# One closing barrier in place of two, and a last wait that subtracts its own count, in a row-maximum kernel

## Chip, cores, metric

One core of one Trainium2 chip. The metric is the device time of the core in microseconds. Beside it stands the span of the profile, which is the time from the first to the last instruction that the profile draws; the two differ. Every run in this document is on record as of the fast state, with a granted TensorE clock of 1.0, which is full speed.

## The reference

```python
def setup_inputs():
    return {"x": np.random.randn(8192, 8192).astype(np.float32)}

def reference(x):
    return np.linalg.norm(x, ord=np.inf, axis=1)
```

That is the largest absolute value of each of the 8192 rows: 268 MB to read, 32 KB to write.

## The kernel before

SyncE issues all loads, VectorE reduces each tile with an absolute maximum, and two stores write the result: the large part's from the queue of ScalarE (ACT) while the last tiles come in, the tail's from SyncE after the last reduction.

```python
        if j == len(LAST) - 4:
            ins = nc.scalar.dma_start(out=out_b, in_=r_bulk[:])     # semaphore 102
            after(ins, done, mybir.DependencyClass.Sync)
    nc.sync.dma_start(out=out_t, in_=r_tail[:])                     # semaphore 103
    nc.at_finalize(start_first_load_early)
    nc.at_finalize(finish_on_pool)
```

```python
def finish_on_pool(nc):
    sp, pool = mybir.EngineType.SP, mybir.EngineType.Pool
    body, end = nc.main_func.blocks[-2:]
    ...                                   # find the last store's semaphore: lane
    insts = end.instructions
    src = next(i for i in insts if i.engine == sp)
    at = next(k for k, i in enumerate(insts) if type(i).__name__ == "InstISA")
    drain, clear = insts[at - 1], insts[at]
    ...
    waits = sorted(src.sync_info.on_wait, key=lambda s: s.id == lane)
    wait = mybir.InstDrain(
        name=nc.get_next_instruction_name(), engine=pool, ins=[], outs=[],
        sync_info=mybir.SyncInfo(on_wait=waits, on_update=[]),
    )
    moved = {src.name, drain.name, clear.name}
    end.instructions = [i for i in insts if i.name not in moved] + [wait, clear]
```

The build splits this wait for nine semaphores into four waits for two semaphores each and a drain that waits for the ninth, VectorE's count (99). The view of line bacc.py:44 shows the four (43 ns each).

Of the kernel before, what the change touches and what calls it, by code (L numbers as in the profile page):

```python
# [62 lines left out]
                return  # L63


def finish_on_pool(nc):



    sp, pool = mybir.EngineType.SP, mybir.EngineType.Pool  # L70
    body, end = nc.main_func.blocks[-2:]
    last_store = [
        i
        for i in body.instructions
        if i.engine == sp and type(i).__name__ == "InstDMACopy"
    ][-1]
    lane = last_store.sync_info.on_update[0].id
    insts = end.instructions
    src = next(i for i in insts if i.engine == sp)
    assert type(src).__name__ == "InstDrain" and not src.sync_info.on_update  # L80
    at = next(k for k, i in enumerate(insts) if type(i).__name__ == "InstISA")
    drain, clear = insts[at - 1], insts[at]
    assert drain.engine == clear.engine == pool
    assert type(drain).__name__ == "InstDrain"
    assert not (drain.sync_info and drain.sync_info.on_wait)
    waits = sorted(src.sync_info.on_wait, key=lambda s: s.id == lane)
    assert waits[-1].id == lane
    wait = mybir.InstDrain(
        name=nc.get_next_instruction_name(),
        engine=pool,  # L90
        ins=[],
        outs=[],
        sync_info=mybir.SyncInfo(on_wait=waits, on_update=[]),
    )
    moved = {src.name, drain.name, clear.name}
    end.instructions = [i for i in insts if i.name not in moved] + [wait, clear]


@with_exitstack
def kernel(  # L100
# [101 lines left out]
    nc.sync.dma_start(out=out_t, in_=r_tail[:])  # L202
    nc.at_finalize(start_first_load_early)
    nc.at_finalize(finish_on_pool)


# [28 lines left out]
```

## Time and profile before

| | |
|---|---|
| time, median of the first 3 runs | 627.68 us (627.46 to 627.82) |
| span of the profile | 625.7 us |
| loads' queue, share of the 16 DMA engines' span | 99.5% |
| VectorE busy | 88% |
| last store: issue, landing | 624.049, 625.469 us |

In the profile's lines POOL is GpSimd, SP SyncE, ACT ScalarE, DVE VectorE and PE the tensor engine (PEld its weight loads); a q behind the name is the engine's sequencer, to which the views give the drains, the waits, the clears and the DMA issues, and L and a number is a source line. The page is read from the top: the share of the engines, the share of the DMA queues, then the chain that ended last; after that the last microseconds one instruction at a time. The prediction below shows those lines. Two lines are added here. The first is from the view of waits and says what VectorE waited for (total us, times, longest): the loads, and nothing else of size (the next entry is 0.9 us).

```profile
DVE r_bulk L140 <- DMA t<-in_x_dram: 69.7, 24, 21.0
```

The second pair is from the view of one source line, the line to which all barrier instructions belong (count, durations in ns, first and last start in us). SyncE's two drains are its entries into the two closing barriers, 0.36 us apart; the first took 123 ns, behind the store's issue, and the second 7.

```profile
L230 SPq DRAIN  x2: 7/65/123, 624.5 to 624.8; - x2
L230 SPq EVENT_SEMAPHORE  x2: 17/17/17, 624.7 to 625.0; - x2
```

No printed view lists the semaphores' updates. They are in the trace, and where the text gives three decimals of a microsecond they are read from its records one by one.

### The profile page before, as it was taken

What the parts mean: (1) busy time and instruction counts of PE and PEld (TensorE: products, weight loads), DVE (VectorE), ACT (ScalarE), POOL (GpSimd) and SP (SyncE); (2) the same over time, 40 slices, a digit from 0 to 9 for tenths busy, and PEclk for the clock granted to TensorE, in tenths of its full rate; (3) what the DMA queues carried; (4) which work ended last, traced back from release to release, by engine and by line L of the source; (5) the groups of instructions that cost most, each with busy time, mean ns of one, the idle gap of its engine ahead of it and who ended that gap; (6) DMA issues with size and microseconds to landing.
All of it is one profiled execution on the core that took longest, in us unless ns stands there. A gap on an engine that the chain in (4) does not pass through costs nothing.

```text
span 625.7 us, 205 instructions
## 1 busy us (share of the span) xinstructions
DVE 552.9 (88%) x67; POOL 0.2 (0%) x4
## 2 busy tenths in 40 slices
DVE  0588988889988889888898888988889999999998
POOL 0000000000000000000000000000000000000000
DMA  9999999999999999999999999999999999999997
GB/s 402 469 402 452 419 452 419 448 423 436 436 419 452 411 461 402 469 402 469 402 469 402 461 411 452 419 448 423 444 413 421 444 425 431 436 425 430 424 422 315
DMA packets 9282, 268.49 MB, mean 429 GB/s; under 512 B 1856, under 2 KB 1856, under 8 KB 3392
## 3 DMA queue, kind: packets, MB, share of 16 engines
q1 hardware_dynamic: 8496, 268.45, 99.5%
q10 hardware_dynamic: 784, 0.02, 0.1%
q14 instruction: 2, 0.02, 0.0%
HBM read 268.44 MB, written 0.03 MB: 429 GB/s over the span
## 4 chain that ended last, share of the span: by engine, by line
DMA 67%; DVE 31%; issue 1%; another core or an unknown queue 0%; DVEq 0%; SPq 0%
DMA t<-in_x_dram 67%; DVE r_bulk L140 24%; DVE part L140 6%; DVE t L140 2%; DVEq L230 0%; DVE r_tail L140 0%; SPq L159 0%
## 5 line engine op out<-in xcount | busy, mean ns | idle before, releaser
L140 DVE TENSOR_REDUCE r_bulk<-t 128x2 f32<-128x16384 f32 x24 | 413.3, 17220 | 69.7 <-DMA t<-in_x_dram 69.7
L140 DVE TENSOR_REDUCE part<-t 128x1 f32<-128x8192 f32 (+20 forms) x28 | 121.5, 4410 | 0.3 <-DMA t<-in_x_dram 0.3
L140 DVE TENSOR_REDUCE t<-t 128x1 f32<-128x1664 f32 (+8 forms) x11 | 16.7, 1576 | 0.2 <-DMA t<-in_x_dram 0.2
L140 DVE TENSOR_REDUCE r_tail<-t 128x1 f32<-128x644 f32 (+1 forms) x2 | 1.5, 814 | 0.0
L137 DVE MEMSET part<- 128x56 f32 x1 | 0.1, 105 | 0.9 <-PEq L219 0.9
L140 DVE TENSOR_REDUCE r_tail<-part 128x14 f32<-128x56 f32 x1 | 0.2, 201 | 0.0
L219 POOL MEMSET const-bfloat16-1.0<- 128x1 bf16 x1 | 0.1, 101 | 0.0
L219 POOL MEMSET const-uint8-127<- 128x1 uint8 x1 | 0.1, 101 | 0.0
L219 POOL MEMSET const-float32-0.0<- 128x1 f32 x1 | 0.1, 98 | 0.2 <-issue 0.2
L219 POOL MEMSET const-float32-1.0<- 128x1 f32 x1 | 0.1, 98 | 0.0
## 6 DMA issues: line engine op xcount, KB each, us to landing
t<-in_x_dram SPq DMA_DIRECT2D x2, 3392.0 KB, 37.2
t<-in_x_dram SPq DMA_DIRECT2D x1, 5376.0 KB, 40.5
t<-in_x_dram SPq DMA_DIRECT2D x1, 4864.0 KB, 32.9
t<-in_x_dram SPq DMA_DIRECT2D x1, 4800.0 KB, 32.9
t<-in_x_dram SPq DMA_DIRECT2D x1, 4672.0 KB, 34.7
t<-in_x_dram SPq DMA_DIRECT2D x3, 1536.0 KB, 36.9
t<-in_x_dram SPq DMA_DIRECT2D x1, 3520.0 KB, 42.7
t<-in_x_dram SPq DMA_DIRECT2D x1, 3328.0 KB, 40.4
```

The source lines that it names most:

```text
L137: nc.vector.memset(part[:], 0.0)
L140: return nc.vector.reduce_max(out=o, in_=i, axis=X, apply_absolute_value=True)
L219: nc = _bacc.Bacc("TRN2", target_bir_lowering=False, num_devices=1)
```

## The change

The intent: end the kernel as soon as the last store has landed. One barrier goes, GpSimd waits only for semaphores that no other instruction has already waited for at their last value (the two stores), clears all others while the last store is in flight, and the wait for that store takes its own 128 off.

```diff
-    waits = sorted(src.sync_info.on_wait, key=lambda s: s.id == lane)
-    wait = mybir.InstDrain(... on_wait=waits ...)
+    met = {}
+    for i in body.instructions:
+        for s in i.sync_info.on_wait if i.sync_info else []:
+            met[s.id] = max(met.get(s.id, 0), s.wait_value)
+    waits = [s for s in src.sync_info.on_wait if met.get(s.id, 0) < s.wait_value]
+    last = [s for s in waits if s.id == lane]
+    others = [s for s in waits if s.id != lane]
 ...
+    tail = [wait([s], []) for s in others]
+    for a, b in ((lo, lane - 1), (lane + 1, hi)):
+        if a <= b:
+            tail.append(clear_range(nc, clear, a, b))
+    reset = mybir.SyncUpdate(sync_type="semaphore", id=lane, ...,
+        update_mode="sem-sub-imm", update_value=last[0].wait_value)
+    tail.append(wait(last, [reset]))
-    moved = {src.name, drain.name, clear.name}
-    end.instructions = [i for i in insts if i.name not in moved] + [wait, clear]
+    end.instructions = [i for i in insts[: at - 1] if i.name != src.name] + tail
```

(Cut: assertions, the arguments that `...` stands for, `clear_range`, which copies the clear with another range, and `wait`, which builds a waiting instruction on GpSimd. `insts[: at - 1]` is the closing block up to the end of its first barrier.)

## The prediction

> **What bounds the kernel now.** I read the page first, then the chain of work that ended last, then the last five microseconds in order of time, and then the records of the closing instructions and of the semaphores one by one. The page:

> ```profile
> span 625.7 us, 205 instructions
> DVE 552.9 (88%) x67; POOL 0.2 (0%) x4
> ...
> q1 hardware_dynamic: 8496, 268.45, 99.5%
> ...
> HBM read 268.44 MB, written 0.03 MB: 429 GB/s over the span
> ...
> DMA 67%; DVE 31%; issue 1%; another core or an unknown queue 0%; DVEq 0%; SPq 0%
> ```

> The loads fill the 16 DMA engines for 99.5% of the span: 268.4 MB have to come in, and nothing in the change touches a load or a reduction. So some 622 of the 625.7 us are out of its reach, and only what follows the last load can move. The end of the chain of waits and the last instructions in order of time (columns: start, duration, what):

> ```profile
> 622.48 0.59 DVE r_tail L140
> 623.07 0.08 issue
> 623.15 0.87 DVEq L230
> ```

> ```profile
> 621.73 0.41 ACTq L200 DMA_DIRECT2D out_dram<-r_bulk  x1
> 622.48 1.55 DVE L140 TENSOR_REDUCE r_tail<-t 128x1 f32<-128x644 f32 x2
> 624.05 0.35 SPq L202 DMA_DIRECT2D out_dram<-r_tail  x1
> ```

> The last reduction ends at 622.48 + 1.55 = 624.03 us, and SyncE starts the last store at 624.05. The chain as printed stops there, with VectorE; it does not follow the store. The list of DMA issues does, from issue to landing:

> ```profile
> out_dram<-r_tail SPq DMA_DIRECT2D x1, 8.0 KB, 1.4
> ```

> The semaphore records make that exact: the sixteenth and last increment of this store's semaphore (103) comes at 625.469, 1.42 us after its issue. Beside it run the closing barriers, here by line and engine (durations in ns, then first and last start in us):

> ```profile
> L230 POOLq EVENT_SEMAPHORE  x4: 17/17/17, 624.6 to 625.0; - x4
> L230 PEldq EVENT_SEMAPHORE  x2: 51/51/51, 624.7 to 625.1; - x2
> L230 POOLq EVENT_SEMAPHORE_RANGE_CLEAR  x1: 92/92/92, 625.6 to 625.6; - x1
> ```

> ```profile
> bacc.py:44 POOLq EVENT_SEMAPHORE  x4: 43/43/43, 625.1 to 625.5; - x4
> ```

> One by one: the first barrier is gathered by GpSimd at 624.601 and released at 624.680; the second is gathered at 624.929 and released at 625.007, so it costs 0.328 us. GpSimd's four waits for pairs of semaphores start at 625.103, 625.195, 625.281 and 625.492; then comes a drain that waits for VectorE's count, which has no record, and the clear from 625.642 to 625.734, which is the end of the span. The fourth wait is the one that held: the three before it follow each other at about 0.09 us, so it would have started at about 625.37, but it started at 625.492, 23 ns after the last increment of semaphore 103. The store's landing, not the barriers, released the end, with about 0.12 us to spare.

> [...] the fourth wait is recorded as 43 ns, although GpSimd stood at it for about 0.12 us. So I read waits from starts and not from durations. [...] This store took 1.42 us for 8 KB and the other one 2.0 us[...]; its own packets run from 624.890 to about 625.10, and the increments come 0.2 to 0.4 us later. [...] semaphore 2 moves at 625.347 and 625.381, then not until 626.261, then four times at 23 to 99 ns; the resets run from 626.446 to 627.109. The pause ends 0.527 us after GpSimd's clear. So the runtime's closing part most likely stands waiting for GpSimd, and what ends GpSimd earlier ends the run earlier by as much.

> **The change part by part.**

> 1. The second closing barrier goes: eight instructions on the other four engines and three on GpSimd. On GpSimd alone it costs 0.328 us, but all of it lies between 624.68 and 625.07, while the store is in flight until 625.469. Worth on the path: 0.

> 2. GpSimd's waits for eight DMA semaphores and VectorE's count become two, those of the two stores. The three waits that pass at once (3 x 0.09 = 0.27 us) also lie before 625.469: 0. The drain for VectorE's count stands behind the landing: it goes, and with it most of the stretch from 625.492 to 625.642 (0.150 us).

> 3. The range clear (0.092 us on record) goes from behind the landing to before it, split in two, for 99 to 102 and 104 to 107. After the only barrier GpSimd is free at about 624.76; the first store's semaphore was complete at 623.726, so this wait passes at once, and two clears at about 0.1 us end near 625.0. That is 0.47 us before the landing: 0.

> 4. The last wait, for semaphore 103, takes its own count off. It should start where the fourth wait starts now, 23 ns after the landing, at 625.492, and the barrier waits of GpSimd that wait and subtract take 17 ns. So it ends at about 625.51, where the kernel before ended at 625.734: 0.225 us less. Counted by spacing instead, GpSimd's own instructions in the barrier follow each other at 79 to 81 ns, so the next could start at about 625.57, against 625.734 or a little later: 0.16 us or more.

> Sum: 0 + 0 + 0 + 0.16 to 0.24; I take 0.20 us. The time is 627.68 - 0.20 = 627.48 us, that is 0.03% less. In front of the last reduction nothing moves: the instruction streams of all five engines are the same up to the closing block, line numbers apart.

> **The rivals.** First, the barrier is on the path after all: a reader who adds up what is removed gets 0.328 + 0.27 + 0.24 = 0.84 us and 626.84 us. Against it speaks the fourth wait's start 23 ns behind the landing. It would hold in part if the store landed early in other executions: the 0.12 us of spare is all that could then show in the time before.

> Second, the runtime's barrier is held by something other than GpSimd's last instruction, for instance by a fixed piece of work, [...]that starts when the barrier ends. Of the pause to 626.261, 0.527 us lie behind the clear, while the first other engine signed 0.28 us after the second barrier, so GpSimd's tail is about 0.25 us longer and I cannot see what is in it. Then the gain would be 0 (627.68 us), or up to the 0.33 us by which the other engines now arrive earlier (627.35 us).

> Third, the shift is lost in the spread: the three runs before span 627.46 to 627.82 us, 0.36 us, more than the gain. [...] I think this is what the plain times will look like: no difference that three runs can tell.

> Fourth, a loss: a subtracting wait, or clears while a store is in flight, slow the store or GpSimd. The clears leave 103 alone, and semaphore updates of the barriers run beside the store's packets today, so I give it little.

> **Range and chances.** The centre is 627.48. The spread of three runs gives 0.2 us either way around a median, another session may add as much, and the rivals reach from 626.84 to about 627.7. I take 627.05 to 627.9. Two per cent would be 12.6 us, sixty times the gain; no rival comes near it, so within 2% gets 0.994, and the rest is split.

> **What would show it right or wrong.** The loads' queue should still be at 99.5%, and the last store should issue about 0.02 us after the last reduction and land 1.4 us later. The increments of semaphore 103 should be followed within about 25 ns by its fall to zero, and the clears of 99 to 102 and 104 to 107 should come before them, near 624.9 to 625.0. Semaphore 2's pause should end sooner after the landing: it was 626.261 - 625.469 = 0.79 us, and I expect about 0.59. If that difference stays at 0.79, the second rival holds; if the landing itself comes later after the issue, the fourth.

> One trap in reading it: the two clears and the last wait are built without a source position, as the drain without a record was, and the span is taken over instructions that have one. So I expect the page to print a span of about 624.8 us (the tensor engine's barrier wait, 624.734 + 0.051) and 205 - 11 - 4 - 1 = 189 instructions. Of that fall of 0.95 us only about 0.2 us is time; the rest is a tail that is no longer drawn. The run's time, not the span, decides. I am wrong if fast runs of the two kernels side by side differ by more than about 0.5 us either way.

The marks stand for cuts: general statements about records, transfers and the steps behind a kernel that were not read from this case's traces, a cause given for the spread that no run tested, and a kind of work named in the second rival. 0 + 0 + 0 + 0.16 to 0.24 us, taken as 0.20, is worked out from the trace alone. What the text calls the runtime's closing part is a group of updates at the end of the trace, described with the result. That it waits for GpSimd was inference from one number, the pause that ends 0.527 us after GpSimd's clear.

## The result

| | before | changed |
|---|---|---|
| time, median of 6 runs | 627.51 us (627.37 to 627.82) | 627.46 us (627.23 to 627.83) |
| ratio | | 0.9999 (95%: 0.9986 to 1.0012) |
| span of the profiled run | 625.7 us | 624.7 us |
| time of the profiled run | 627.57 us | 627.34 us |

A ratio is the mean time of one kernel's fast runs over the mean of the other's in the same rounds, so it is not quite the ratio of the medians in the table. By the plain times the two kernels can't be told apart. The changed kernel's page (header, queues, chain):

```profile
span 624.7 us, 189 instructions
DVE 553.0 (89%) x67; POOL 0.2 (0%) x4
...
q1 hardware_dynamic: 8352, 268.44, 99.6%
...
DMA 67%; DVE 31%; issue 1%; another core or an unknown queue 0%; DVEq 0%; SPq 0%
```

The end in order of time (start, duration, what), and the last store's issue (KB, us to landing):

```profile
622.39 1.55 DVE L180 TENSOR_REDUCE r_tail<-t 128x1 f32<-128x644 f32 x2
623.97 0.35 SPq L242 DMA_DIRECT2D out_dram<-r_tail  x1
```

```profile
out_dram<-r_tail SPq DMA_DIRECT2D x1, 8.0 KB, 1.4
```

And the closing instructions (the line of the barrier):

```profile
L270 POOLq EVENT_SEMAPHORE  x2: 17/17/17, 624.5 to 624.6; - x2
L270 SPq EVENT_SEMAPHORE  x1: 17/17/17, 624.6 to 624.6; - x1
L270 PEldq EVENT_SEMAPHORE  x1: 51/51/51, 624.7 to 624.7; - x1
```

The loads, the reductions and the store are as they were. One barrier is left, and the drawing ends with it at 624.7 us, before the store has landed (625.394): the clears and the last wait are missing from the page. So the one microsecond by which the span fell must not be taken for time.

The semaphores' records show the rest. At the end of the trace stand updates that no drawn instruction makes; they are called the runtime's here. In the kernel before, semaphore 2 moves nine times (625.347 to 626.546 us), the semaphores from 7 to 255 are reset (248 of these 249 on record, 626.446 to 627.109), and semaphore 2 moves nine times more (627.333 to 627.690: 0.357 us, as in the changed kernel, with 23 to 99 ns from one to the next). I take each nine for a barrier over the five engines and call its updates signatures; the experiments below find four of the engines among the first five. In both profiled runs the run time ends 0.12 us before the last signature is on record (627.57 against 627.690, 627.34 against 627.464), so I let the last signature stand for the end of the run; the difference is 0.11 to 0.13 us in all thirteen profiled runs of this document. Everything is given from the landing of the last store, the sixteenth increment of semaphore 103:

| us after the landing | before | changed |
|---|---|---|
| last wait starts | 0.023 | not drawn |
| last reset of the kernel's own semaphores | 0.238 | 0.049 |
| third signature | 0.792 | 0.602 |
| ninth signature | 1.077 | 0.886 |
| tenth signature (after the runtime's reset) | 1.864 | 1.713 |
| eighteenth and last signature | 2.221 | 2.070 |

The closing part became 0.190 us shorter up to the third signature, and 0.151 us in all: between the ninth and the tenth signature 0.827 - 0.787 = 0.040 us were given back. The rest of the 0.23 us between the two profiled runs is a landing that happened to come 0.075 us earlier.

### The profile page after: what moved, and what is told of

Its sections match the earlier page's. It is cut to its first block, busy times and chain, and to the rows that moved or that the text cites. A ratio compares the mean times of both kernels' runs of the same rounds, so it can differ in the third digit from the quotient of the medians.

```text
span 624.7 us, 189 instructions
## 1 busy us (share of the span) xinstructions
DVE 553.0 (89%) x67; POOL 0.2 (0%) x4
## 3 DMA queue, kind: packets, MB, share of 16 engines
q1 hardware_dynamic: 8352, 268.44, 99.6%
HBM read 268.44 MB, written 0.03 MB: 430 GB/s over the span
## 4 chain that ended last, share of the span: by engine, by line
DMA 67%; DVE 31%; issue 1%; another core or an unknown queue 0%; DVEq 0%; SPq 0%
DMA t<-in_x_dram 67%; DVE r_bulk L180 24%; DVE part L180 6%; DVE t L180 2%; DVEq L270 0%; DVE r_tail L180 0%; SPq L199 0%
```

## The experiments

Eleven more runs were made, ten of new kernels and one of the changed kernel again, all with a correct result. Each states its edit against the changed kernel unless said otherwise; from the second on, edits to that kernel also carry the marks of the first. Times are medians; "before" is the kernel before in the same rounds.

### Drawing what the page left out

```diff
-def clear_range(nc, clear, first, last):
+def clear_range(nc, clear, first, last, line):       # debug=mark(clear, line)
-    def wait(waits, updates):
+    def wait(waits, updates, line=903, engine=pool): # debug=mark(clear, line)
-    for a, b in ((lo, lane - 1), (lane + 1, hi)):
+    for a, b, line in ((lo, lane - 1, 901), (lane + 1, hi, 902)):
```

(`mark` copies a source position with another line number; the comments stand for an argument that both functions pass on.)

> The changed kernel with source positions given to its three undrawn closing instructions (marked L901 and L902 for the clears, L903 for the last wait), nothing else. If the short span of the changed kernel's page (624.7 us, 189 instructions) is only a tail that was not drawn: 192 instructions, a span that ends about 0.04 us after the last store's landing, so about 625.4 us, and a run time minus span of about 1.9 us where the changed kernel showed 2.64; run time within 627.2 to 627.9 like the changed kernel. From landing to the runtime's next signature on semaphore 2: 0.60 us as before the drawing. If instead the changed kernel really ended at 624.7: the span stays near 624.7. If the positions themselves cost time: landing to signature other than 0.60.

The header of its page, and the three marked lines (view by source line):

```profile
span 625.9 us, 192 instructions
```

```profile
L901 POOLq EVENT_SEMAPHORE_RANGE_CLEAR  x1: 55/55/55, 625.2 to 625.2; - x1
...
L902 POOLq EVENT_SEMAPHORE_RANGE_CLEAR  x1: 47/47/47, 625.2 to 625.2; - x1
...
L903 POOLq EVENT_SEMAPHORE  x1: 17/17/17, 625.9 to 625.9; - x1
```

Time 627.63 us (627.27 to 627.88), before 627.50; ratio 0.9999 (0.9985 to 1.0014). The three instructions are there, and the span is the changed kernel's plus a tail. In this run the store landed at 625.855, later than expected, because the last reduction ended later too; the wait starts 0.023 us behind it and the span ends at 625.895, 0.040 behind it. Landing to the third signature is 0.602 us. Run time minus span is now 1.87 to 1.95 us in the four runs, where the undrawn kernel had 2.59 to 2.67 in its six. The fall of the span was a fall of what is drawn. The clears lie at 625.155 and 625.236, 0.70 and 0.62 us ahead of the landing. The wait for the first store is no line of its own: in the trace the first clear (L901) carries it.

### The second barrier put back

```diff
-    end.instructions = [i for i in insts[: at - 1] if i.name != src.name] + tail
+    moved = {src.name, drain.name, clear.name}
+    end.instructions = [i for i in insts if i.name not in moved] + tail
```

> The changed kernel with the second closing barrier put back in front of the clears. Theory (a barrier in the shadow of the store's landing costs nothing): GpSimd reaches its last wait about 0.33 us later, at about 0.2 us before the landing instead of 0.55; landing to signature stays at 0.60 us and the run time does not change. Rival (barriers add up): landing to signature 0.93 us and the run 0.33 us longer.

The second clear (view by source line; the span of this run is 626.0 us):

```profile
L902 POOLq EVENT_SEMAPHORE_RANGE_CLEAR  x1: 47/47/47, 625.7 to 625.7; - x1
```

The store lands at 625.960 here, so the clears come 0.3 us closer to it, as expected, and it does not matter: third signature at 0.603 us. Time 627.58 us (627.28 to 627.88), ratio 0.9998 (0.9981 to 1.0014). The rival's 0.93 us is refuted. One thing was not expected: the ninth to the tenth signature takes 0.787 us, so this kernel's last signature comes at 2.034, earlier than the changed kernel's 2.070.

### The kernel before with one barrier

The edit is against the kernel before:

```diff
+        debug=mark(clear, 904),
-    end.instructions = [i for i in insts if i.name not in moved] + [wait, clear]
+    end.instructions = [i for i in insts[: at - 1] if i.name not in moved] + [wait, clear]
```

> The kernel before with its second barrier taken out and everything else left: four paired waits, the drain that waits for the vector engine's count (now with a source position, L904), then the clear of all. Theory: the barrier was hidden, so landing to signature stays at 0.79 us and the drain's place, between the fourth wait at about 0.02 us after the landing and the clear 0.15 us later, is seen for the first time. Rival (barriers add up): 0.79 - 0.33 = 0.46 us and the run 0.33 us shorter.

```profile
L904 POOLq EVENT_SEMAPHORE  x4: 43/43/43, 625.1 to 625.9; - x4
L904 POOLq DRAIN  x1: 34/34/34, 626.0 to 626.0; - x1
```

The landing is at 625.841. The fourth wait starts at 625.865, the drain at 625.951, the clear at 626.015: the two steps that the change removed from behind the landing, 0.086 and 0.064 us from start to start. Third signature at 0.793 us: taking the barrier away by itself moves nothing there, and the rival's 0.46 is refuted. From the ninth to the tenth it takes 0.829 us, the longer value again, and the last signature comes at 2.264. Time 628.09 us (627.72 to 628.21) against 627.50, ratio 1.0006 (0.9991 to 1.0021). The 0.04 us explain little of that; in the profiled run the rest lies in front of the last reduction's end (624.387 us, before: 624.021), which the edit does not touch. In all four runs the excess lies inside the span: time minus span is 1.89 to 1.92 us, beside 1.80 to 1.89 before. The interval holds 1, and I leave that part open.

### The clear put back behind the last wait

```diff
-    for a, b, line in (...):  tail.append(clear_range(...))
-    tail.append(wait(last, [reset]))
+    tail += [wait(last, []), clear]
```

> The changed kernel with one clear of all nine semaphores put back behind the last wait, without the drain and without the subtraction. It splits the 0.19 us that the change took from landing to signature. Theory: the wait starts 0.02 us after the landing, the clear follows at about 0.085 us (GpSimd's spacing in the barrier) and not at 0.15, its last semaphore falls about 0.07 us after its start, so landing to signature is about 0.73 us: 0.13 us of the gain is the clear, 0.06 us the drain. Rival (the drain is the dear part, the clear is nearly free because it overlaps the way out): 0.60 to 0.65 us. Rival (the drain is free and the clear is all of it): 0.79 us.

```profile
L903 POOLq EVENT_SEMAPHORE  x1: 17/17/17, 625.4 to 625.4; - x1
```

```profile
L267 POOLq EVENT_SEMAPHORE_RANGE_CLEAR  x1: 92/92/92, 625.5 to 625.5; - x1
```

Wait at 625.429, clear at 625.495, landing at 625.406. Third signature at 0.708 us, between the two rivals and 0.02 us under my figure, since the clear followed the wait after 0.066 us and not 0.085. So of the 0.190 us, 0.792 - 0.708 = 0.084 were the drain's place and 0.708 - 0.602 = 0.106 the clear's; I had said 0.06 and 0.13. Time 627.70 us (627.46 to 627.78), ratio 1.0000 (0.9986 to 1.0015).

### Four more barriers, as a control

If the barrier is free because it lies in a shadow, enough of them must leave it. The closing block's barrier was copied four times (mark L905) in front of the clears. (`barrier` makes the copy.)

```diff
+    more = [i for _ in range(4) for i in barrier()]
-    end.instructions = [i for i in insts[: at - 1] if i.name != src.name] + tail
+    end.instructions = [i for i in insts[: at - 1] if i.name != src.name] + more + tail
```

> The changed kernel with four more barriers like the remaining one, in front of the clears: a control in which barriers must become visible. In the drawn run GpSimd would have reached its last wait 0.54 us before the landing, and one more barrier brought it 0.33 us nearer. Theory (only what outlasts the landing counts): four barriers put it 4 x 0.33 - 0.54 = 0.79 us behind the landing, so landing to signature is 0.60 + 0.77 = 1.37 us and the run 0.77 us longer. Rival (every barrier costs its 0.33 us): 1.92 us and the run 1.3 us longer. Rival (barriers never show): 0.60 us.

```profile
L905 POOLq EVENT_SEMAPHORE  x8: 17/17/17, 625.0 to 626.1; - x8
...
L903 POOLq EVENT_SEMAPHORE  x1: 17/17/17, 626.4 to 626.4; - x1
```

The landing is at 625.533, and the last wait starts at 626.367: now the barriers are what the end waits for. Third signature at 1.412 us (expected 1.37; the third copy took 0.371 us in place of 0.328). The 0.81 us more are less than the four barriers' 1.35, by about 0.54 us of slack; the rival of 1.92 us is refuted, and so is the thought that barriers never show. Time 628.09 us (627.98 to 628.26) against 627.64, ratio 1.0006 (0.9992 to 1.0020): even 0.62 us at the last signature is hardly told by four runs.

### The last wait on another engine

```diff
-    tail.append(wait(last, [reset]))
+    tail.append(wait(last, [reset], engine=sp))
```

> The changed kernel with its last wait, and the subtraction, on SyncE in place of GpSimd; GpSimd still makes the two clears. In the traces so far GpSimd signs the runtime's barrier 0.58 us after its last wait begins, but the first signer, which is the tensor engine, signs 0.285 us after its own. Theory (GpSimd's way out is longer than the others', and SyncE is the last of the five to sign, so the four before it sign while the store flies): the signature that follows the landing comes at about 0.31 us and is the fifth, where the changed kernel has its fifth at 0.67; landing to the last signature of all 1.71 us in place of 2.07, and the run 0.36 us shorter than the changed kernel, 0.5 us shorter than before. Rival (any engine that ends last needs 0.58 us): fifth at 0.60, the run 0.07 us shorter.

```profile
L903 SPq EVENT_SEMAPHORE  x1: 17/17/17, 625.6 to 625.6; - x1
```

Landing at 625.621, wait at 625.638. The third and fourth signatures, which stood behind the landing until now, come at -0.043 and +0.001 us, before or just at the landing and ahead of the last wait; the fifth comes at 0.178 us, earlier than the 0.31 of the theory and far from the rival's 0.60. The last comes at 1.529 us. Time 626.89 us (626.84 to 627.22) against 627.64, ratio 0.9988 (0.9975 to 1.0000).

The same with `engine=mybir.EngineType.Activation`, which is ScalarE:

> The same with the last wait on the scalar engine, which the traces take for the second signer. Theory (GpSimd's long way out is its own): second signature about 0.31 us after the landing and the fifth at about 0.41, so 0.26 us shorter than the changed kernel and 0.10 us longer than with SyncE. Rival (any engine that ends last needs 0.58 us): second at 0.60 and the fifth at 0.71, 0.04 us longer than the changed kernel.

```profile
L903 ACTq EVENT_SEMAPHORE  x1: 17/17/17, 625.3 to 625.3; - x1
```

Second signature at 0.178 us, fifth at 0.284, last at 1.684; time 627.13 us (626.88 to 627.79), ratio 0.9992 (0.9978 to 1.0006). So the order of signing is seen: ScalarE is second, GpSimd third, SyncE fifth, because each time that one was the first to come late. And the way from the start of the last wait to the own signature is 0.161 us on SyncE, 0.157 on ScalarE and 0.579 on GpSimd (in the drawn kernel, 625.878 to 626.457). GpSimd's long way out is its own, and it does not hang on the wait: in the run with SyncE, where GpSimd ends with a clear, its signature (the third) comes 0.573 us after that clear begins. What fills it is not drawn and stays open.

### Where the 0.04 us went

In the first six traces (before, changed, and the first four experiments) the ninth to the tenth signature took 0.787 us in both kernels with two barriers and 0.826 to 0.829 in the four with one. The records of the reset show where. They fall into the groups 207 to 255, 156 to 206, 105 to 155, 54 to 104 and 7 to 53 (in the kernel before from 626.446, 626.563, 626.601, 626.615 and 626.762 us on). The semaphores 7 to 53 are reset last, up to 0.224 us before the tenth signature in the kernel before as in the changed one, and their first reset came 0.542 to 0.546 us behind the third signature in those four, 0.501 and 0.502 in those two. By the order of signing (the tenth is the first signature of the runtime's second barrier) I take these to be the tensor engine's, as an expectation below does; no record names the engine. It has two closing instructions fewer with one barrier. Two drains that wait for nothing (mark L906) give their number back:

```diff
+    pad = [mybir.InstDrain(name=..., engine=mybir.EngineType.PE, ins=[], outs=[], debug=mark(clear, 906))
+           for _ in range(2)]
-    end.instructions = [i for i in insts[: at - 1] if i.name != src.name] + tail
+    end.instructions = [i for i in insts[: at - 1] if i.name != src.name] + pad + tail
```

> The changed kernel with two drains that wait for nothing put on the tensor engine after the barrier, in place of the two instructions that it lost. With one barrier the runtime's reset of the semaphores[...] took 0.827 us from the ninth signature to the tenth in the four traces, with two barriers 0.787 in both. Theory (the place of the code behind, after two fewer instructions, costs 0.04 us there): back to 0.787 and landing to the last signature 2.03 in place of 2.07. Rival (it is the longer wait of the tensor engine before the landing that does it): stays at 0.827. The run's time can't show 0.04 us.

```profile
L906 PEldq DRAIN  x2: 7/8/8, 625.3 to 625.3; - x2
```

Third signature 0.603 us, ninth to tenth 0.786, last at 2.032: the 0.04 us are back. The first signature moves too, from 0.456 us ahead of the landing in the drawn kernel to 0.306 here and 0.131 with the four drains below, so the first signer is the tensor engine. The time is 627.55 us (627.29 to 627.92), ratio 0.9997 (0.9982 to 1.0012), and shows nothing, as expected. With four drains:

> The changed kernel with four empty drains on the tensor engine in place of two. If the 0.04 us depend on where the following code falls in groups of four instructions, four are like none: ninth to tenth signature 0.827 us. If any two or more instructions do it (the control with eight more also had 0.788): 0.787 us, or a new value. In the run's time nothing of this can be seen.

Ninth to tenth 0.784 us, last at 2.029; 627.45 us in two runs. So it is not a matter of groups of four: 2, 4 or 8 instructions more than the changed kernel (8 in the control) all give 0.784 to 0.788, and none gives 0.826 to 0.830. The length of the tensor engine's wait is not it either: from its signature to the ninth it waited 1.20 us in the kernel before and 0.80 in the one with SyncE, and the former had 0.787, the latter 0.830; and the control, which waited 0.79, had 0.788. So at least two more closing instructions on that engine are shown to take the 0.04 us away, by one trace of each kernel; why, is open.

### Both together, and the changed kernel once more

> Both findings together: the last wait on SyncE, and two empty drains on the tensor engine. If they add up: fifth signature 0.18 us after the landing as with SyncE alone, ninth to tenth signature 0.787 us in place of 0.830, landing to the last signature 1.49 us in place of 1.53 with SyncE alone, 2.07 in the changed kernel and 2.22 before. The run about 0.7 us shorter than before and 0.6 us shorter than the changed kernel in the same rounds: near 626.8 us. If the tensor engine's reset is not what the runtime's second part waits for once SyncE signs early: 1.53 us.

```profile
L903 SPq EVENT_SEMAPHORE  x1: 17/17/17, 626.0 to 626.0; - x1
```

Fifth signature 0.177 us behind the landing (625.941), ninth to tenth 0.788, last at 1.485: they add up. Time 626.82 us (626.65 to 627.30) against 627.55 for the kernel before, ratio 0.9988 (0.9974 to 1.0001). From landing to last signature it is 2.221 - 1.485 = 0.736 us shorter, and the medians differ by 0.73. This is the fastest version seen.

> The changed kernel itself, unaltered, beside the kernel before and the combination in the same rounds. Theory: landing to the last signature 2.07 us again, 0.15 us less than before, which five rounds with a spread of 0.4 us can't show: a ratio within 0.001 of 1. Rival (the change is worth the 0.84 us that the removed instructions add up to): ratio 0.9987.

Third signature 0.602, last 2.071; 627.43 us (627.24 to 627.67), ratio 0.9997 (0.9985 to 1.0010). The interval holds both the theory's 0.9998 and the rival's 0.9987; its centre lies by the theory, but what refutes the rival is the trace, and below the spans of the runs, not the plain times.

All closing parts, us from the last store's landing; the last column is explained below the table:

| kernel | 3rd | 5th | 9th to 10th | last | end by all runs (runs) |
|---|---|---|---|---|---|
| before | 0.792 | 0.859 | 0.787 | 2.221 | 2.10 (25) |
| before, one barrier | 0.793 | 0.860 | 0.829 | 2.264 | 2.17 (4) |
| changed | 0.602 | 0.669 | 0.827 | 2.070 | 1.95 (6) |
| changed, drawn | 0.602 | 0.670 | 0.828 | 2.071 | 1.94 (4) |
| changed again | 0.602 | 0.670 | 0.828 | 2.071 | 1.93 (5) |
| with second barrier | 0.603 | 0.670 | 0.787 | 2.034 | 1.92 (4) |
| clear behind | 0.708 | 0.775 | 0.826 | 2.176 | 2.04 (4) |
| four more barriers | 1.412 | 1.479 | 0.788 | 2.842 | 2.73 (4) |
| two drains on tensor | 0.603 | 0.670 | 0.786 | 2.032 | 1.89 (4) |
| four drains on tensor | 0.603 | 0.670 | 0.784 | 2.029 | 1.94 (2) |
| last wait on ScalarE | 0.216 | 0.284 | 0.826 | 1.684 | 1.54 (4) |
| last wait on SyncE | -0.043 | 0.178 | 0.830 | 1.529 | 1.40 (5) |
| SyncE and two drains | -0.029 | 0.177 | 0.788 | 1.485 | 1.35 (5) |

Three traces of the changed kernel agree to 0.001 us here, while run times spread over several tenths. The spread sits inside the span: in nine runs of the kernel before beside the control, the time ran from 627.40 to 628.23 us and the time minus the span only from 1.80 to 1.88.

That gives a check on more than one trace of each kernel, since the record lists the span of every run in it but those of the kernel before beside the result. The last column adds two things: the mean of time minus span over these runs of a kernel, and the span's end, counted from the landing, in its trace (0.265 us for the kernel before, 0.040 for the changed one drawn, -0.687 undrawn). It is an estimate, as it takes that second part for the same in all runs of a kernel, and spans are listed to 0.1 us. It lies 0.09 to 0.14 us under the last signature everywhere, as the end of the profiled runs does (0.11 to 0.13). So the change is worth 0.16 us by 25 and 15 runs (the trace: 0.151), SyncE's wait 0.70 against before (0.692), both together 0.76 (0.736). The steps of 0.04 us are too small for this check.

## Why the prediction was right, and where it was not

- The second barrier, priced at 0: right. Put back it left the third signature at 0.603, taken away alone it left it at 0.793. The control shows that the price is 0 only within about 0.54 us of slack.
- The three early waits, priced at 0: consistent with the traces. In the kernel before they end ahead of the landing (the third starts at 625.281 and takes 43 ns; the landing is at 625.469); they were not varied by themselves.
- The drain and the clear, priced together at what lay between the fourth wait and the end of the span: right in sum, 0.190 us against 0.16 to 0.24, split 0.084 and 0.106.
- The new clears, priced at 0 because they end ahead of the landing: right; in the drawn kernel they start 0.70 and 0.62 us ahead of it, and the last wait 0.023 us behind it. Two signs were off without harm: the clears had been put at 0.47 to 0.57 us ahead, and the fall of semaphore 103 within 0.025 us of its last increment is on record only after 0.049.
- "what ends GpSimd earlier ends the run earlier by as much": this step was right in kind and failed in size. The run's end moved by 0.151 us and not 0.190, just under the stated range of the gain. Taking a barrier away also takes two instructions from the tensor engine, and the resets that I take for its own then start 0.04 us later (0.542 against 0.501 us behind the third signature). The prediction had called the streams the same up to the closing block and looked no further than the barrier on semaphore 2.
- The rival of a runtime barrier that something other than GpSimd holds: refuted by its own sign, since the pause after the landing did not stay at 0.79 us but fell to 0.602. With the last wait on another engine the fifth signature comes 0.39 and 0.49 us earlier still. The prediction had noted that GpSimd's tail was longer than the first signer's, and did not follow it up; that tail was worth more than the whole change.
- The rival of a loss from clears while a store is in flight: not seen; issue to landing was 1.420 us before and 1.426 after, and 1.42 to 1.43 in all thirteen traces.
- The span, foretold at 624.8 us with 189 instructions: 624.7 and 189.
- The time: 627.48 us foretold, 627.46 measured. That they agree to 0.02 us is luck: in the six runs the kernel before had itself come down from 627.68 to 627.51, which is more than the gain.
- That three runs would not tell the difference: right for plain times, and nor did six, nor five more. The record shows only that the spread lies inside the span.
- A slip in reading: behind its pause semaphore 2 moves seven times (626.261 to 626.546 us), 23 to 99 ns apart, and not four; three of these fall among the first resets. Nothing in the sum rests on it.

## What to carry to other kernels

Before counting what is removed from a closing sequence, find the one event that it waits for at the end, here a store's landing, and price only what stands behind it. If the gain sought is smaller than the spread of the run time, measure an interval in the trace that starts at that event, prove with a control that the interval would show the cost, and see whether time minus span shows it over all runs. Then ask which engine should stand at the last wait: here that choice gave 0.54 us and the change under study 0.15.
